# Rearranging loads and side work in an encoder-layer kernel: transform spectra and twiddles per frequency group, filter work out of the out-projections, filter network first, first loads in stages

## The chip, the cores and the metric

The kernel runs on all eight cores of one Trainium2 chip, one batch element per core, without any traffic between cores. The metric is the device time of the slowest core, in microseconds (us). A program on all eight cores has a second, slower state in some executions, in which the cores of one die, or of both, show a lower granted clock and the time is some per cent longer. Each run is labelled fast or slow, and only fast runs, or the undisturbed die of a run, are compared here. Times of fast runs repeat within about 0.3%.

## The reference, cut to what matters

One encoder layer on `x` of 2048 tokens by 2048 channels per core:

```python
x = x + 0.5 * swiglu(rmsnorm(x), w_ff1_in, w_ff1_out)        # FF1, 5632 hidden
h = rmsnorm(x)
proj = h @ w_in                # q/k/v of 6 heads, Hyena's v/x1/x2, memory queries, 3 gates
y_a = dilated sliding-window attention(...)                   # 3 groups of 2 heads
y_b = hyena_mixer(...)         # twice: multiply by x1/x2 after a long FFT convolution
y_c = cross attention into 256 memory tokens
merged = sig(ga)*(y_a @ w_br_a) + sig(gb)*(y_b @ w_br_b) + sig(gc)*(y_c @ w_br_c)
x = x + merged @ w_out
x = rmsnorm(x + 0.5 * swiglu(rmsnorm(x), w_ff2_in, w_ff2_out))  # FF2, closing norm
```

The long convolutions use filters that a small network of sine layers makes from positions alone. Their spectra depend on weights only, so the kernel computes them beside FF1, long before they are used.

## The kernel before

The kernel is a recorder: Python calls append operations in program order, every operation gets the semaphore waits that its data needs, and each engine then runs its own operations in that order. DMAs that the code gives to `"sp"` go out on one queue, in order; if one of them has to wait, everything behind it waits too. `"pool"` issues the weight loads.

Matmuls of the layer's large products are the main work. Everything else that needs the tensor engine (memory keys, filter spectra, attention, the Hyena operator) is a generator, a *side*, of which one step is recorded now and then between main matmuls. `rate` is the number of side steps per tick; a tick comes about every 8 to 16 main matmuls.

```python
    def tick(self):
        ...
        self.credit = min(self.credit + self.rate, 2.0) if self.sides else 0.0
        while self.credit >= 1.0 and self.sides:
            self.credit -= 1.0
            self.step()                       # one step of the first side in the list
```

The filter side: network, first transform step, and the second step that this excerpt shows. `T.tw` holds the twiddles, `T.ks` the spectra in HBM: a spectrum is the transform of a filter, and the twiddles are constant matrices that the second step of a transform, or of its inverse, multiplies with. The third component of a spectrum repeats the first.

```python
        seq2 = [(th, fg) for th in range(3) for fg in range(16)]
        def wload(i):
            th, fg = seq2[i]
            P.dma("sp", tw[i % 3][:], T.tw[fg][:, 0:3, :])
            P.dma("sp", W[i % 4]..., T.vk[o][th][:, 8 * fg:8 * fg + 8]...)
        for i, (th, fg) in enumerate(seq2):
            ... 4 matmuls into one bank ...
            wload(i + 3)
            P.store(0, T.ks[o][th][fg][:, 0:2, :], k_[:])
            P.store(0, T.ks[o][th][fg][:, 2, :], k_[:, 0, :])
            yield
```

The Hyena side, for each of two orders: a first step, 48 products (3 channel blocks `th` by 16 frequency groups `fg`) with a forward and an inverse part, and the inverse's last step (`last`) with 24 tiles. "Twiddle phase" below means the 48 products of an order. `W` is the result of the first step, `K` a spectrum, `Z` what the last step reads, `zz` its result.

```python
    W = bufs(P, "f_W", 4, [128, 2, 256], BF16, B)
    tw = bufs(P, "f_tw", 4, [128, 6, 128], BF16, B + 4 * KB)
    K = bufs(P, "f_K", 4, [128, 3, 256], F32, B + 10 * KB)
    zz_ = ring(bufs(P, "f_zz", 2, [128, 512], F32, B + 24 * KB))

    def fload(o, i):
        th, fg = i // 16, i % 16
        P.dma("sp", W[i % 4][:], T.vu[o][th][:, 8 * fg:8 * fg + 8]...)   # 128 KB
        P.dma("sp", K[i % 4][:], T.ks[o][th][fg])                        # 384 KB
    def tload(i):
        P.dma("sp", tw[i % 4][:], T.tw[i % 16])                          # 192 KB
    ...
        for i in range(50):                       # order(o)
            if i < 48:
                q.append((i, fwd(o, i)))
                yield
            if i >= 2:
                n, Y = q.pop(0)
                inv(o, n, Y)                      # stores 128 KB
                yield
            fload(o, i + 3)
            tload(i + 2)
    ...
        def zl(c6):                               # last(o): rows of 128 bf16, 256 bytes
            for part in range(2):
                P.dma("sp", Z[c6 % 2][:, part], T.vz[o][th][part][:, :, cc * 128:(cc + 1) * 128])
        for n, (c6, tb) in enumerate(its):        # 24 tiles
            ... 8 matmuls of 128 columns ...
            P.stt(zz[:], ps[:, bank, :], 2.0 / NFFT, v[:], ALU.mult, ALU.add)
            if o == 0:
                P.tt("dve", zz[:], zz[:], x[:], ALU.mult)
                P.store(1, T.z1[c6][:, tbs(tb)], zz[:])      # zz is busy until this lands
            ld(n + 3)                             # two loads of 256 KB
            yield
```

The start, and where the sides run in FF1:

```python
        for i in range(8):
            xload(i)                              # x tiles, 256 KB each
        W1.issue(2)                               # 2nd and 3rd FF1 weight tile, 1 MB each
        ... three weight tiles by four token blocks ...
        P.side("memkv", side_memkv(C, P, T, SIDE))
        P.side("filter", side_filter(C, P, T, SIDE))
        P.rate = 1.0                              # in in-projections and out-projections
```

## Time and profile before

| | |
|---|---|
| time, median of the runs | 6,091 us (6,084 to 6,103, four fast runs) |
| matmul work at full pace | about 5,605 us |
| lost on the slowest core | about 496 us |

*Lost* is used throughout: the length of a stage less its matmuls at full pace. A stage runs from the first matmul of its kind to the first of the next. The full pace is read from dense stretches: 465 matmuls of 512 columns in 100 us, 0.215 us each (over 4,640 such matmuls in a row it is 0.2158 us, and the losses in the tables below are reckoned with that); shorter matmuls count by their columns, with a floor of 0.06 us. The few fp32 matmuls are counted by their columns too, although the trace records 0.6 to 0.9 us for one of 512 columns, and so show a little as lost. Busy time of the tensor engine hides these losses, because a slow matmul is busy too.

Lines of the page of the kernel before. The last line counts DMA packets; the one before it has the granted clock of the tensor engine in tenths, in 40 slices of the span:

```profile
span 6101.1 us, 79583 instructions; the slowest of 8 cores (6032.7 to 6101.1 us)
PE 5767.4 (95%) x27356; PEld 2659.6 (44%) x27356; DVE 2166.2 (36%) x3185; ACT 1251.0 (21%) x2064; POOL 753.6 (12%) x876
PEclk9999999999999999999979989999999999999999
DMA packets 505331, 792.29 MB, mean 130 GB/s; under 512 B 94151, under 2 KB 274119, under 8 KB 493639
```

The windows view of the kernel before, core 4. Columns: stretch in us and its length, busy us (and instructions) of PE, weight loads, DVE, ACT, POOL, then granted clock, mean busy share of the DMA engines, GB/s. The stretches are FF1's first out-projection, its second in-projection, the q/k projection, the gate stage that holds most of the Hyena side, a dense stretch, and within the gate stage's surroundings the first twiddle phase and the first last step:

```profile
514.00:798.00 284.00, 258.69 (x1172) 114.01 (x1172) 85.02 (x128) 35.11 (x60) 7.91 (x15) 0.96 0.96 264
798.00:1295.00 497.00, 485.81 (x2317) 222.29 (x2315) 185.97 (x283) 99.56 (x171) 8.44 (x16) 0.99 0.65 169
2276.00:2517.00 241.00, 206.57 (x979) 92.85 (x977) 150.16 (x224) 130.14 (x218) 89.59 (x83) 0.95 0.40 87
2837.00:3720.00 883.00, 719.39 (x3643) 356.95 (x3642) 371.17 (x550) 199.76 (x337) 226.29 (x281) 0.88 0.70 181
3800.00:3900.00 100.00, 100.00 (x465) 45.36 (x464) 43.80 (x64) 13.21 (x21) 5.27 (x10) 1.00 0.41 94
2754.00:3039.00 285.00, 243.94 (x1247) 125.00 (x1245) 148.98 (x216) 64.36 (x109) 96.98 (x127) 0.93 0.76 205
3039.00:3181.00 142.00, 75.06 (x473) 40.30 (x472) 45.94 (x68) 45.92 (x80) 10.74 (x12) 0.76 0.79 183
```

The out-projection has its DMA engines busy 96% of the time; the gate stage takes 883 us for 3,643 matmuls, and its clock is 0.88 on average. Most of this low clock is a consequence of gaps and not their cause: the Trainium skill, "TensorE: Matmul & The Clock Gate", Part 1, says that the clock falls to half after an idle window and needs a busy one to come back, and this trace agrees (0.76 in the last step with its many gaps, 1.00 in the dense stretch; core 4 has 260 us at 0.5 in all). The exception is a stretch from 3,551 to 3,713 us in which cores 4 and 5 ran mostly at 0.812, a value that no other core of this run shows. Who the tensor engine waited for, from the waits view (us in total, times, longest):

```profile
PE P L225 <- DVE f_zz_246 L249: 32.1, 8, 16.5
PE P L225 <- DMA f_tw_220<-c_tw: 27.2, 9, 6.5
PE P L225 <- DVE f_zz_247 L249: 21.9, 4, 7.1
PE P L225 <- DMA h_W_124<-vk_s: 19.0, 8, 5.8
PE P L225 <- DMA h_W_123<-vk_s: 18.9, 7, 5.6
PE P L225 <- DMA f_Z_236<-vz_s: 18.1, 5, 9.4
...
PE P L225 <- ACT q_sq_159 L240: 17.3, 2, 16.5
```

`f_tw` are the twiddles (70 us over the four buffers), `h_W` the filter side's inputs, `f_zz` and `f_Z` belong to the last step, `q_sq` is the start of the q/k stage, where the cos/sin tables come late.

### The profile page before, as it was taken

What the parts mean: (1) busy time and instruction counts of PE and PEld (TensorE: products, weight loads), DVE (VectorE), ACT (ScalarE), POOL (GpSimd) and SP (SyncE); (2) the same over time, 40 slices, a digit from 0 to 9 for tenths busy, and PEclk for the clock granted to TensorE, in tenths of its full rate; (3) what the DMA queues carried; (4) which work ended last, traced back from release to release, by engine and by line L of the source; (5) the groups of instructions that cost most, each with busy time, mean ns of one, the idle gap of its engine ahead of it and who ended that gap; (6) DMA issues with size and microseconds to landing.
All of it is one profiled execution on the core that took longest, in us unless ns stands there. A gap on an engine that the chain in (4) does not pass through costs nothing.

```text
span 6101.1 us, 79583 instructions; the slowest of 8 cores (6032.7 to 6101.1 us)
## 1 busy us (share of the span) xinstructions
PE 5767.4 (95%) x27356; PEld 2659.6 (44%) x27356; DVE 2166.2 (36%) x3185; ACT 1251.0 (21%) x2064; POOL 753.6 (12%) x876
## 2 busy tenths in 40 slices
PE   7999889999999998898858889999999999999998
PEld 3444444444444453444424434444444444444443
DVE  3345225322332216665434443422222122322325
ACT  3211112110002445542232211123000000000014
POOL 0000000000002303302303311023000000000015
PEclk9999999999999999999979989999999999999999
DMA  7327974687225714367777764455212642156334
GB/s 162 65 48 197 268 209 119 179 223 186 39 38 135 182 52 97 87 160 208 202 182 206 197 152 96 94 152 150 42 35 48 180 108 42 35 133 164 66 91 166
DMA packets 505331, 792.29 MB, mean 130 GB/s; under 512 B 94151, under 2 KB 274119, under 8 KB 493639
## 3 DMA queue, kind: packets, MB, share of 16 engines
q1 hardware_dynamic: 456472, 583.30, 31.4%
q0 software_dynamic: 47232, 203.44, 20.2%
q8 instruction: 226, 3.70, 0.3%
q14 instruction: 169, 1.38, 0.1%
q10 hardware_dynamic: 1232, 0.46, 0.0%
HBM read 730.40 MB, written 260.05 MB: 162 GB/s over the span
## 4 chain that ended last, share of the span: by engine, by line
PE 79%; DMA 10%; SPq 4%; DVE 3%; issue 2%; ACT 2%; POOL 0%; ACTq 0%; DVEq 0%; POOLq 0%
PE P L225 79%; SPq L267 3%; DMA h_W_123<-vk_s 1%; DMA f_tw_220<-c_tw 1%; DMA xT_s<-a_xr_70 1%; DMA h_W_124<-vk_s 1%; DMA f_tw_218<-c_tw 1%; DMA z_s<-f_zz_247 1%; DMA xT_s<-a_xr_72 1%; DMA f_tw_219<-c_tw 0%; DMA x_in_77<-xt 0%; DMA f_tw_221<-c_tw 0%; DMA xT_s<-a_xr_69 0%; DMA z_s<-f_zz_246 0%; DMA vu_s<-f_stg_1_209 0%
## 5 line engine op out<-in xcount | busy, mean ns | idle before, releaser
L225 PE MATMUL P<-HT,a_w_0_62 128*128 128x512 bf16 x2816 | 626.7, 380 | 0.0
L225 PE MATMUL P<-HT,b_w_0_282 128*128 128x512 bf16 x2816 | 611.5, 379 | 0.0
L225 PE MATMUL P<-HT,b_w_1_283 128*128 128x512 bf16 x2816 | 611.4, 379 | 0.0
L225 PE MATMUL P<-HT,a_w_1_63 128*128 128x512 bf16 x2688 | 595.3, 379 | 0.0
L225 PEld LDWEIGHTS P<-HT,b_w_0_282 128*128 128x128 bf16 x2816 | 275.9, 98 | 332.2 <-issue 0.6
L225 PEld LDWEIGHTS P<-HT,b_w_1_283 128*128 128x128 bf16 x2816 | 275.2, 98 | 332.6
L225 PEld LDWEIGHTS P<-HT,a_w_0_62 128*128 128x128 bf16 x2816 | 275.8, 98 | 330.2 <-issue 10.8
L225 PEld LDWEIGHTS P<-HT,a_w_1_63 128*128 128x128 bf16 x2688 | 262.3, 98 | 311.1 <-issue 3.7
L225 PE MATMUL P<-HT,x_w_128 128*128 128x512 bf16 x1344 | 325.7, 394 | 0.0
L225 PE MATMUL P<-a_gT,a_w_0_64 128*128 128x512 bf16 x1408 | 316.4, 383 | 5.7 <-DVE a_xr_72 L249 2.8
L225 PE MATMUL P<-a_gT,a_w_1_65 128*128 128x512 bf16 x1408 | 318.2, 384 | 1.8 <-DMA a_w_1_65<-w_ff_out 1.8
L225 PE MATMUL P<-HT,x_w_129 128*128 128x512 bf16 x1344 | 319.2, 388 | 0.0
L225 PE MATMUL P<-HT,x_w_130 128*128 128x512 bf16 x1280 | 315.8, 397 | 0.0
L225 PE MATMUL P<-HT,x_w_131 128*128 128x512 bf16 x1280 | 311.3, 393 | 0.5 <-DVE m_m_259 L243 0.5
L225 PE MATMUL P<-b_gT,b_w_0_284 128*128 128x512 bf16 x1056 | 230.5, 379 | 0.0
L225 PE MATMUL P<-b_gT,b_w_1_285 128*128 128x512 bf16 x1056 | 230.5, 379 | 0.0
L225 PEld LDWEIGHTS P<-a_gT,a_w_0_64 128*128 128x128 bf16 x1408 | 138.8, 99 | 173.5 <-issue 13.9
L225 PEld LDWEIGHTS P<-a_gT,a_w_1_65 128*128 128x128 bf16 x1408 | 139.3, 99 | 168.7 <-issue 10.3
L225 PEld LDWEIGHTS P<-HT,x_w_128 128*128 128x128 bf16 x1344 | 135.6, 101 | 159.2 <-issue 33.1
L225 PEld LDWEIGHTS P<-HT,x_w_129 128*128 128x128 bf16 x1344 | 133.1, 100 | 152.2 <-issue 21.8
L225 PEld LDWEIGHTS P<-HT,x_w_130 128*128 128x128 bf16 x1280 | 129.4, 102 | 149.9 <-issue 31.2
L225 PEld LDWEIGHTS P<-HT,x_w_131 128*128 128x128 bf16 x1280 | 128.1, 101 | 147.3 <-issue 30.5
(889 smaller groups left out, 6478.5 us busy)
## 6 DMA issues: line engine op xcount, KB each, us to landing
b_w_0_282<-w_ff_in POOLq DMA_DIRECT2D x22, 1024.0 KB, 8.3
b_w_1_283<-w_ff_in POOLq DMA_DIRECT2D x22, 1024.0 KB, 8.3
a_w_1_63<-w_ff_in POOLq DMA_DIRECT2D x21, 1024.0 KB, 9.3
a_w_0_62<-w_ff_in POOLq DMA_DIRECT2D x21, 1024.0 KB, 9.1
x_w_128<-w_in POOLq DMA_DIRECT2D x21, 512.0 KB, 7.3
x_w_129<-w_in POOLq DMA_DIRECT2D x21, 512.0 KB, 8.0
x_w_130<-w_in POOLq DMA_DIRECT2D x20, 512.0 KB, 6.6
x_w_131<-w_in POOLq DMA_DIRECT2D x20, 512.0 KB, 7.3
```

The costliest lines, as they stand in the source:

```text
L225: self.add("pe", lambda e: e.matmul(out, lhsT=lhsT, rhs=rhs, start=start, stop=stop), r=(lhsT, rhs), w=(out,))
L267: self.add(q, lambda e: e.dma_start(out=out, in_=in_), r=(in_,), w=(out,), dma=True, shared=shared)
```

## The change

Its intent: move fewer bytes in the Hyena side, in longer rows, with fewer loads that a matmul waits for; run filter work only where the DMA engines have room; get the first projection going sooner; use the idle start for the filter network. The diff, cut to its core:

```diff
 # filter side: groups outermost, one twiddle load and one store per spectrum
-        seq2 = [(th, fg) for th in range(3) for fg in range(16)]
+        seq2 = [(fg, th) for fg in range(16) for th in range(3)]
-                P.dma("sp", tw[i % 3][:], T.tw[fg][:, 0:3, :])
+                if th == 0:
+                    P.dma("sp", tw[fg % 2][:], T.tw[fg][:, 0:3, :])
-            P.store(0, T.ks[o][th][fg][:, 0:2, :], k_[:])
-            P.store(0, T.ks[o][th][fg][:, 2, :], k_[:, 0, :])
+            P.store(0, T.ks[o][fg, th], k_[:])
 # Hyena side
-    W = bufs(P, "f_W", 4, [128, 2, 256], BF16, B)
-    tw = bufs(P, "f_tw", 4, [128, 6, 128], BF16, B + 4 * KB)
-    K = bufs(P, "f_K", 4, [128, 3, 256], F32, B + 10 * KB)
+    W = bufs(P, "f_W", 2, [128, 2, HYW], BF16, B)            # HYW: all 768 channels
+    tw = bufs(P, "f_tw", 2, [128, 6, 128], BF16, B + 6 * KB)
+    K = bufs(P, "f_K", 4, [128, 2, 256], F32, B + 9 * KB)
-        P.tt("dve", tb[:], pv, k[:, 1:3, :], ALU.mult)
+        P.tt("dve", tb[:, 0, :], pv[:, 0, :], k[:, 1, :], ALU.mult)
+        P.tt("dve", tb[:, 1, :], pv[:, 1, :], k[:, 0, :], ALU.mult)
-        zp = zp_()
+        zp = zp_[fg % 2]
...
-        P.store(1, T.vz[o][th][:, 8 * fg:8 * fg + 8]..., zp[:])
+        if th == 2:
+            P.store(1, T.vz[o][:, :, 8 * fg:8 * fg + 8]..., zp[:]...)
-                for part in range(2):
-                    P.dma("sp", Z[c6 % 2][:, part], T.vz[o][th][part][:, :, cc * 128:(cc + 1) * 128])
+                P.dma("sp", Z[n % 2]..., T.vz[o][th][:, :, 8 * bh:8 * bh + 8, :]...)   # 4 KB rows
                 q.append((i, fwd(o, i)))
+                kload(o, i + 3)
+                if i % 3 == 2:
+                    wload(o, i // 3 + 2)
                 yield
...
                 inv(o, n, Y)
+                if n % 3 == 2:
+                    tload(n // 3 + 2)
                 yield
-            fload(o, i + 3)
-            tload(i + 2)
 # start: the network's first layer among the x tiles, weights 2 and 3 only after x tiles 10 and 15
-        W1.issue(2)
+        P.side("mlp", side_mlp(C, P, T, A + 24 * KB, hh3b))
+        P.step()
...
+        W1.issue(1, also=(C.HT[:, 10, 0:512],))
+        W1.issue(1, also=(C.HT[:, 15, 0:512],))
...
+        P.drain("mlp")                          # its other two layers, all at once
 # FF1: side steps in the in-projections alone
-        P.rate = 1.0
+            P.tag = "ff1.in";  P.rate = 0.87
+            P.tag = "ff1.out"; P.rate = 0.0
 # q/k stage: V is loaded behind the cos/sin tables, attention starts two steps later
-        load_v(P, T, V)
+    load_v(P, T, V)                             # inside mix_qk, after the tables
```

## The prediction

> **What bounds the kernel now.** TensorE. In dense stretches of the windows view (after 3,720 us) 465 matmuls of 512 columns fit into 100 us, 0.215 us each, at granted clock 1.000. All matmuls of the timeline at that pace make about 5,605 us of the 6,101 us span (slowest core, 4). The other ~496 us are idle TensorE and half clock. By stage core 4 loses: before the first projection matmul 38 us; FF1's first in-projection 15; first out-projection (514 to 798 us) 44; second in-projection 24; start of q/k 42; gate stage with the Hyena work (2,837 to 3,720 us) 245, and 16 before it; tail 28. Undisturbed cores lose 200 to 215 us in the gate stage: cores 4 and 5 ran 150 us of it at clock 0.812.
>
> **Causes.** In the first out-projection the DMA engines are 94 to 102% busy (windows, 600 to 800 us), and the waits view has 38 us on filter spectra loads (h_W). In the gate stage it has 70 us on twiddle loads (f_tw), 54 on f_zz, 25 on f_Z. Gaps also halve the clock (mean 0.79 in 3,000 to 3,100 us), as the Trainium skill, "TensorE: Matmul & The Clock Gate", Part 1, says of idle windows; this trace agrees. The inverse transform's last step reads 256-byte runs: 26,000 of 37,000 packets in 3,024 to 3,182 us are under 512 B, the least that "DMA: Bandwidth & Descriptors", Specifications, asks for.
>
> **What the change does, priced.** TensorE work is the same (5,618 us counted in both programs).
> 1. Start: only 4 MB of x and the first weight tile precede the first projection; the next two tiles wait. First projection: 40.6 us becomes about 28. The filter network's later layers form a serial knot (2 us of DVE per block, 4 to 6 us of TensorE idling), repaid by its first layer moving into the idle start. Gain 12.
> 2. Filter work leaves the out-projections; 32.5 us of its matmuls move into in-projections, where DMA is 20 to 50% busy. 44 + 24 us of loss become about 8. Gain 60.
> 3. cos/sin tables load before V: the 16.5 us wait under q_sq mostly goes. Gain 14.
> 4. Hyena, per frequency group: K falls from 3x384 to 3x256 KB, twiddles from 3x192 to 192 KB, three stores become one; 2.5 MB become 1.7 MB. A twiddle load has three steps (about 6 us) of lead instead of two (4 us), against 5 to 6 us median to landing. 106 us of loss there become about 30. The last step's reads become 4 KB runs, but it still moves 1 MB per 2 us step, so it stays DMA-bound: 85 + 38 us become about 70. Expected gain 105, not the ideal 129. Cost: one more DVE product per step, off the chain.
>
> Sum: about 190 us, nearly all on the critical path, because TensorE's chain is the span.
>
> **Predicted: 5,905 us; 5,840 to 5,980 eight times in ten. Faster by over 2%: 0.84; within 2%: 0.14; slower: 0.02.**
>
> **What would show it.** First projection before 32 us; first out-projection about 210 us instead of 283; no h_W entry above 10 us in the waits view; f_tw below 20 us; packets under 512 B from 94,000 to about 45,000; gate stage 720 to 760 us instead of 883; ff2 unchanged.
>
> **What would make it wrong.** Twiddle waits becoming waits for K or W on the one in-order load queue; the filter knot stalling TensorE over 15 us; filter traffic delaying in-projection weights; denser matmuls bringing more of the 0.812 clock.

## The result, and the profile after

The changed kernel took 5,903 and 5,914 us in its two fast runs; two more runs were slow (one die at a clock of 0.81 and 0.85). The ratio of the fast runs to those of the kernel before is 0.970 (95% interval 0.967 to 0.973). Ratios are the mean time of one kernel's fast runs over that of the other's of the same rounds, so they are not quite the ratio of medians that are quoted. The lines that answer to those of before:

```profile
span 5901.2 us, 78600 instructions; the slowest of 8 cores (5877.6 to 5901.2 us)
PE 5712.2 (97%) x27356; PEld 2650.1 (45%) x27356; DVE 2178.8 (37%) x3308; ACT 1251.7 (21%) x2074; POOL 752.7 (13%) x876
PEclk9999999999999999999989999999999999999999
DMA packets 408365, 748.18 MB, mean 127 GB/s; under 512 B 39175, under 2 KB 174087, under 8 KB 396679
```

The windows view of the changed kernel, core 5, for the same stages in the same order:

```profile
528.00:735.00 207.00, 207.00 (x961) 93.84 (x960) 44.90 (x66) 0.40 (x1) 7.91 (x15) 1.00 0.74 203
735.00:1210.00 475.00, 475.00 (x2252) 216.10 (x2251) 184.21 (x279) 90.95 (x155) 8.44 (x16) 1.00 0.51 130
2224.00:2446.00 222.00, 204.31 (x979) 92.59 (x977) 148.87 (x224) 130.21 (x218) 89.09 (x80) 0.98 0.40 94
2754.00:3520.00 766.00, 676.79 (x3660) 347.81 (x3659) 389.66 (x648) 201.51 (x342) 229.48 (x286) 0.93 0.68 181
3600.00:3700.00 100.00, 100.00 (x466) 45.34 (x464) 43.53 (x63) 13.46 (x22) 5.28 (x10) 1.00 0.42 96
2698.00:2939.00 241.00, 226.79 (x1228) 120.38 (x1226) 150.32 (x259) 61.89 (x105) 98.93 (x129) 0.97 0.72 185
2939.00:3068.00 129.00, 81.03 (x471) 41.34 (x470) 45.45 (x67) 46.44 (x81) 7.82 (x10) 0.76 0.79 203
```

The out-projection has lost nothing any more, and the first twiddle phase is 44 us shorter with the same number of matmuls within 2%. The first last step is hardly shorter: 129 us against 142, with its clock still at 0.76. The waits view of the changed kernel:

```profile
PE P L225 <- DVE f_zz_240 L249: 19.1, 7, 8.9
PE P L225 <- DMA h_z<-c_zT: 17.0, 1, 17.0
PE P L225 <- DVE f_zz_241 L249: 14.2, 5, 4.5
...
PE P L225 <- DMA a_w_1_63<-w_ff_in: 5.3, 1, 5.3
...
PE P L225 <- DMA f_tw_216<-c_tw: 4.8, 3, 3.3
...
PE P L225 <- DMA f_tw_215<-c_tw: 2.9, 4, 1.0
```

Twiddle waits fell from 70 to 8 us and there is no `h_W` entry left. New are `h_z` (the filter network's table, at the very start) and a second FF1 weight tile that comes late. The other signs that the forecast named came too: packets under 512 B fell to 39,175, and the table has the first projection at 29 us, the first out-projection at 207 us, the gate stage at 755 us (median) and no change in FF2.

By stage, median of the eight cores from the traces, length in us and in brackets what is lost of it:

| stage | before | changed | best of the experiments |
|---|---|---|---|
| start, to the first projection matmul | 40.0 (37.5) | 29.0 (24.7) | 30.0 (26.6) |
| FF1, first in-projection | 473.7 (15.7) | 496.8 (30.8) | 469.7 (14.7) |
| first out-projection | 283.1 (44.0) | 207.2 (0.0) | 207.2 (0.1) |
| second in-projection | 489.9 (18.9) | 475.6 (9.8) | 476.5 (10.0) |
| second out-projection | 210.7 (1.9) | 207.2 (0.0) | 207.2 (0.0) |
| third in-projection | 386.8 (0.0) | 421.9 (3.3) | 437.3 (7.1) |
| q/k projection | 240.6 (42.1) | 223.9 (25.4) | 223.4 (24.9) |
| Hyena projection, second half | 191.7 (19.8) | 179.2 (9.0) | 182.5 (12.3) |
| gates of branches A and C, with the Hyena side | 851.4 (213.0) | 754.6 (114.5) | 677.1 (37.1) |
| everything after | unchanged within 5 us | | |
| third out-projection, memory queries and V, Hyena projection's first half | changed by 3 us or less each | | |

The Hyena side's phases, in the same way, add the detail that the stages hide:

| | twiddles, order 0 | last step, order 0 | twiddles, order 1 | last step, order 1 |
|---|---|---|---|---|
| before | 278.7 (54.6) | 134.1 (78.6) | 251.4 (48.1) | 83.0 (37.2) |
| changed | 237.9 (14.3) | 123.8 (68.8) | 211.1 (7.3) | 61.6 (15.4) |

### The profile page after: what moved, and what is told of

It is laid out like the page before. It is cut to its first block, busy times and chain, and to the rows that moved or that the text cites. A ratio compares the mean times of both kernels' runs of the same rounds, so it can differ in the third digit from the quotient of the medians.

```text
span 5901.2 us, 78600 instructions; the slowest of 8 cores (5877.6 to 5901.2 us)
## 1 busy us (share of the span) xinstructions
PE 5712.2 (97%) x27356; PEld 2650.1 (45%) x27356; DVE 2178.8 (37%) x3308; ACT 1251.7 (21%) x2074; POOL 752.7 (13%) x876
## 2 busy tenths in 40 slices
DMA packets 408365, 748.18 MB, mean 127 GB/s; under 512 B 39175, under 2 KB 174087, under 8 KB 396679
## 4 chain that ended last, share of the span: by engine, by line
PE 87%; DMA 7%; DVE 3%; ACT 1%; issue 1%; POOL 0%; SPq 0%; DVEq 0%; ACTq 0%; POOLq 0%
PE P L225 87%; DMA z_s<-f_zz_241 1%; DMA xT_s<-a_xr_70 1%; DMA xT_s<-a_xr_73 0%; DMA xT_s<-a_xr_72 0%; DMA xT_s<-a_xr_71 0%; DMA hyx_s<-y_uc_191 0%; POOL R L243 0%; DMA f_tw_216<-c_tw 0%; SPq L267 0%; DMA f_tw_215<-c_tw 0%; DMA f_zv_232<-z_s 0%; DMA vu_s<-f_stg_0_207 0%; DMA vz_s<-f_zp_229 0%; DMA xT_s<-a_xr_69 0%
## 5 line engine op out<-in xcount | busy, mean ns | idle before, releaser
L225 PE MATMUL P<-a_gT,a_w_0_64 128*128 128x512 bf16 x1408 | 311.1, 382 | 5.1 <-DMA a_w_0_64<-w_ff_out 5.1
L225 PE MATMUL P<-a_gT,a_w_1_65 128*128 128x512 bf16 x1408 | 307.8, 379 | 1.3 <-DMA a_w_1_65<-w_ff_out 1.3
```

What stands on the lines that cost most here:

```text
L225: self.add("pe", lambda e: e.matmul(out, lhsT=lhsT, rhs=rhs, start=start, stop=stop), r=(lhsT, rhs), w=(out,))
```

## The experiments

Twelve kernels ran, all correct against the reference. Whole-kernel times of fast runs are few, because many runs fell in the slow state; the stages of a trace, mostly over four to eight undisturbed cores (two in h_tw48lead), carry most verdicts. The kernel before took 6,052 to 6,103 us in its fast runs on the different chips, and the changed kernel itself ran on the first chip alone, so whole-kernel times from different rounds compare only within some 50 us.

### Parts undone, one at a time

**u_hyena.** The changed kernel with the old Hyena side, and the spectra stored as before.

```diff
-def side_hyena(...):  ... the changed one ...
+def side_hyena(...):  ... the one of before, with T.vu, T.vz, T.ks shaped as before ...
-            P.store(0, T.ks[o][fg, th], k_[:])
+            P.store(0, T.ks[o][th][fg][:, 0:2, :], k_[:])
+            P.store(0, T.ks[o][th][fg][:, 2, :], k_[:, 0, :])
```

> The changed kernel with the Hyena part alone put back (three-component spectra, twiddles per product, 256-byte rows in the inverse's last step). Theory: this part is worth about 105 us, nearly all in the gate stage: gate stage about 850 us again on the median core instead of 755, whole kernel about 6,005 us, ratio to the kernel before about 0.986; FF1 stages as in the changed kernel within 10 us. Rival (the gate stage got shorter because the stages before it hand over in a better state, not because of the loads): gate stage below 800 us.

Two fast runs: 6,003 and 6,006 us. The profiled run was slow on die 0; on the four undisturbed cores the gate stage took 850.0 us against 754.6 and the Hyena projection's second half 187.9 against 179.2, together 104 us. The theory holds: the gain goes and comes with the Hyena part itself; the stages before it, which this run keeps as changed, did not make it. The ratio was a miss: 0.992 against the one fast run of the kernel before in these rounds (6,052 us), where 0.986 was expected. The waits view of core 4 of this run has the old waits back:

```profile
PE P L225 <- DMA f_tw<-c_tw: 58.5, 22, 6.9
PE P L225 <- DVE f_zz L249: 44.5, 13, 20.2
```

**u_filter.** Filter work in the out-projections again, with the filter's own traffic still cut.

```diff
-            P.rate = 0.87      # in-projections
-            P.rate = 0.0       # out-projections
+        P.rate = 1.0           # once, before the loop
```

> The changed kernel with filter work allowed in the out-projections again (one step per tick everywhere), its loads still cut to one twiddle per group and one spectrum store. Theory of place (the out-projection's own x traffic and the filter's traffic together are more than the DMA engines carry): first out-projection loses 30 to 45 us again beyond its matmuls, kernel 30 to 45 us slower than the changed one. Rival of amount (the cut in the filter's own traffic did it): loss under 12 us there, kernel within 12 us of the changed one.

The first out-projection took 274.9 us and lost 42.4, as before the change; fast runs were 5,934, 5,936 and 5,967 us. Over all of FF1 the median core was 40 us slower than the changed kernel (39 without cores 0 and 1, which ran 300 us of it at a clock of 0.812). So the place is worth 40 us. That the filter's smaller traffic is worth nothing does not follow: since the network is done earlier here, this out-projection holds all 192 matmuls of the first order's second transform step, against 116 in the kernel before, and loses no more. No run has the old traffic in the new place. (The edit also raises the rate in the in-projections from 0.87 to 1.0.) The windows view of an undisturbed core (6), for this stage, shows the DMA engines as full as in the kernel before:

```profile
525.00:800.00 275.00, 246.91 (x1177) 116.18 (x1175) 56.86 (x87) 33.45 (x57) 8.45 (x16) 0.96 0.92 259
```

**u_loadv.** V ahead of the tables again.

```diff
+        load_v(P, T, V)        # before the q/k stage
-    load_v(P, T, V)            # in it, after the tables
-    for _ in range(4):
+    for _ in range(2):
```

> The changed kernel with the V loads ahead of the cos/sin tables again and attention starting two steps sooner. Theory: the q/k stage becomes about 17 us longer (224 to 241 us on the median core) and the kernel about 17 us slower. Rival (the wait only moves to the attention that needs V): kernel within 5 us.

The profiled run was slow on die 0. On die 1 the q/k stage was 236.8 us (223.9 in the changed kernel), the first half of the Hyena projection 130.4 (127.7), its second half 173.7 (179.2). So 13 us came back where expected, 3 more right after, and 5.5 were returned later, probably because attention that starts two steps sooner leaves less behind: 10 us net. The theory holds for the stage and is two thirds right for the kernel. The one fast run (5,907 us) can't show 10 us.

**u_weights.** The second and third weight tile at once.

```diff
+        W1.issue(2)
-        W1.issue(1, also=(C.HT[:, 10, 0:512],))
-        W1.issue(1, also=(C.HT[:, 15, 0:512],))
```

> The changed kernel with the second and third FF1 weight tiles loaded at once again. Theory A (holding them back is what brought the first projection from 40 to 29 us): first projection at 36 us or later, no wait for the second tile, start plus first in-projection within 5 us of the 526 us of the changed kernel, because the 5 us wait for the second tile goes in return. Theory B (the x loads are held by the filter network's first step in VectorE's order, not by the weights): first projection moves by less than 4 us and the stage gets about 5 us shorter.

The first projection started at 40.2 us instead of 29.0, and start plus first in-projection took 529.8 us instead of 525.8: theory A. Holding the weights back brings the first matmul 11 us forward and 4 us in the end. Fast runs were 5,902, 5,904 and 5,910 us, no different from the changed kernel.

### What in the Hyena side did it

The change did three things to the twiddle phases at once: 256 KB less per product, loads that cover a group instead of a product, and more lead for each. Four runs separate them.

**h_bytes** puts the bytes back as loads that nothing reads.

```diff
             P.dma("sp", K[i % 4][:], T.ks[o][i // 3, i % 3])
+            P.dma("sp", more[i % 4][:], T.hyx[i % 4][:, tbs(i % 4)])     # 256 KB
```

> The changed kernel, and beside every spectrum load a further load of 256 KB that nothing reads: the bytes that the change took out of the two twiddle phases are back, and no matmul waits for them. In the changed kernel these phases lose 22 us beyond their matmuls (238 and 211 us long), in the kernel before 103 us (279 and 251). Theory of bytes (fewer bytes, so shorter landings, so no stalls): the loss is back at 70 us or more. Theory of deadlines (one twiddle load per group with three steps of lead instead of one per product with two): loss under 45 us.

The two phases lost 86 us (49.0 + 37.1), of 103 in the kernel before and 22 in the changed one. Fast runs were 5,956 to 5,974 us, ratio 0.982. This is what the theory of bytes expected.

**h_tw48** loads twiddles once per product again, two steps ahead.

```diff
-    tw = bufs(P, "f_tw", 2, [128, 6, 128], BF16, B + 6 * KB)
+    tw = bufs(P, "f_tw", 4, [128, 6, 128], BF16, zoff)
-                if n % 3 == 2:
-                    tload(n // 3 + 2)
                 yield
+            tload(i + 2)                        # tw[i % 4] <- T.tw[i // 3]
```

> The changed kernel with the twiddles loaded once per product again, in four buffers and issued two steps ahead as before; spectra, inputs and stores stay as changed. It adds 128 KB per product, half of what the run with dead loads adds. Theory of deadlines: twiddle waits of 40 us or more in the waits view and a loss of 60 to 90 us in the two phases. Theory of bytes: at most half of the loss that the dead loads bring.

The phases lost about 61 us on the four undisturbed cores (32.8 + 28.8), with half of the bytes of h_bytes. That is more than half of what h_bytes lost above the changed kernel (39 of 64 us), so neither theory alone fits both runs. The waits view, first of h_bytes, then of h_tw48 (core 3):

```profile
PE P L225 <- DMA f_tw<-c_tw: 54.0, 16, 8.1
```

```profile
PE P L225 <- DMA f_tw<-c_tw: 37.5, 24, 4.4
```

In both it is the twiddles that are late: few and long waits in the first, many and short in the second. The question is then whether they are late because the engines are full or because the load has too little lead. Two more runs changed only the lead.

**h_tw48lead** is h_tw48 with six buffers (the diff is cut, and against h_tw48). Counted in the code, two steps of lead become six, not the eight that the expectation says.

```diff
-    tw = bufs(P, "f_tw", 4, ...)      tload(i + 2)
+    tw = bufs(P, "f_tw", 6, ...)      tload(i + 4)
```

> Twiddles per product again, as in the run that lost 61 us in the two phases (22 in the changed kernel) with 37 us of twiddle waits, the same bytes, but six buffers and four products (about eight steps) of lead instead of two. Theory (per-product loads cost mostly through their short lead): twiddle waits under 5 us, loss 22 to 35 us. Rival (the 128 KB more per product cost by themselves): loss stays above 50 us, the waits turn up at W or K.

The profiled run was slow, but cores 4 and 5 went slow only at 3,337 us, after both twiddle phases. There the phases lost 16.5 us (12.7 + 3.8), with no wait for twiddles, W or spectra in the waits view of core 4. The windows view of that core has the first phase: as many bytes as in h_tw48, DMA engines 84% busy, and the phase as short as in the changed kernel.

```profile
2693.00:2931.00 238.00, 225.68 (x1249) 120.61 (x1247) 150.60 (x260) 64.10 (x109) 100.25 (x131) 0.98 0.84 220
```

So 128 KB more per product costs nothing, if the twiddles are issued in time. Its one fast run was 5,900 us, against 5,974 for the one of h_tw48 (on another chip, where the kernel before ran within 15 us of the same time). The phases account for 45 of these 74 us; the rest may be the scatter of single runs.

**h_bytelead** is h_bytes with a third twiddle buffer (the diff is cut, and against h_bytes).

```diff
-    tw = 2 buffers; tload(n // 3 + 2)
+    tw = 3 buffers; tload(n // 3 + 3)
```

> The run with the dead loads again (256 KB more per product in the twiddle phases, which then lost 86 us, 54 us of it waiting for twiddles), now with a third twiddle buffer, so that a twiddle load has about nine steps of lead instead of three. Theory: bytes cost time because they make every landing later than its lead; then the twiddle waits vanish (under 5 us) and the loss of the two phases falls to 40 us or less although the bytes are the same. Rival (the DMA engines carry no more, whatever the lead): twiddle waits turn into waits for W or K, and the loss stays above 65 us.

Neither number came. The waits for twiddles vanished, as the theory said, but the loss only fell from 86 to 57 us (33.3 + 23.5), and the next load in line was late instead (13 to 25 us by core; the profiled core 4 below). Fast runs took 5,934 and 5,948 us.

```profile
PE P L225 <- DMA f_W<-vu_s: 24.9, 9, 4.6
```

The windows view of the same core has the first phase:

```profile
2702.00:2964.00 262.00, 231.01 (x1233) 120.61 (x1232) 152.76 (x262) 63.64 (x108) 100.35 (x131) 0.96 0.88 217
```

The DMA engines were 87 and 94% busy in the two phases, against 72% in the changed kernel, and W's 384 KB took a median of 9.8 us to land, against 4.7 to 6.5. With 256 KB more per product the engines are near full, and lead for one stream moves the wait to another. Taken together: bytes and lead are one question, whether a load lands before its use. In these runs lead was enough at 84% busy engines, and not near 90%, where fewer bytes are needed as well. The busy share alone does not set when a load lands: W took a median of 9.1 us in h_bytes at 83%, and 5.3 us in h_tw48lead at 84%. By an estimate the kernel before would have needed both: its first phase shows 76% over 285 us, and the same traffic in the changed kernel's 241 us would be 90% (76 x 285 / 241). The change gave both; no run gave the kernel before more lead alone.

**h_zruns**: the last step's reads as 256-byte rows again, same bytes.

```diff
-                P.dma("sp", Z[n % 2]..., T.vz[o][th][:, :, 8 * bh:8 * bh + 8, :]...)
+                for part in range(2):
+                    for cc in range(2):
+                        cs = slice(cc * 128, cc * 128 + 128)
+                        P.dma("sp", Z[n % 2][:, part, :, cs], T.vz[o][th][part][:, 8 * bh:8 * bh + 8, cs])
```

> The changed kernel with the inverse's last step reading 256-byte runs again, the same bytes. Today the two last steps lose 69 and 15 us (124 and 62 us long); before 79 and 37. Theory of packets: the second comes back to about 35 us and the first to about 79, kernel about 25 us slower. Rival (only the bytes and the order count): both within 6 us of today.

The last steps took 140.3 and 79.5 us (124 and 62 in the changed kernel) and lost 85.0 and 33.3, and fast runs took 5,937 us. The theory of packets holds, with a little more than it forecast. The count of short packets is nearly the kernel before's (94,151) again:

```profile
DMA packets 455022, 748.19 MB, mean 126 GB/s; under 512 B 88903, under 2 KB 223815, under 8 KB 443335
```

The Trainium skill, "DMA: Bandwidth & Descriptors", Specifications, gives 512 B as the least size for full rate. This run agrees: 49,700 more packets under 512 B, at the same bytes, cost 34 us in the two last steps. (It also issues four loads where the changed kernel has one, so a part of the 34 us may be issue.)

### What still bounds the last step

**r_zz4.** In the changed kernel's first last step the DMA engines are 79% busy, so bandwidth is not used up. The waits view of VectorE in that stretch (2,939 to 3,068 us) names another cause:

```profile
DVE f_zz_241 L249 <- DMA z_s<-f_zz_241: 29.7, 7, 6.7
DVE f_zz_240 L249 <- DMA z_s<-f_zz_240: 17.7, 3, 11.7
```

A result buffer can't be written again before its store has landed, and there are two of them. The run gives it four:

```diff
-    zz_ = ring(bufs(P, "f_zz", 2, [128, 512], F32, B + 24 * KB))
+    zz_ = ring(bufs(P, "f_zz", 2, [128, 512], F32, B + 24 * KB) + bufs(P, "f_zzb", 2, [128, 512], F32, B + 31 * KB))
```

> The changed kernel with four instead of two result buffers in the inverse's last step. The forecast held this step to be bound by DMA bandwidth, but in the changed kernel's profile VectorE waits 47 us in it for the store of the buffer that it wants to write again. Theory of buffers: the first order's last step shortens from 124 to 105 us or less, kernel 15 to 25 us faster. Rival (bandwidth): under 6 us shorter, the wait turns up as one for loads.

The first last step fell from 123.8 to 99.3 us, the second, which stores nothing, stayed at 62.0. One fast run: 5,885 us. VectorE's waits for stores fell from 47 to 9 us, and the windows view now shows the step at bandwidth, which it had not been:

```profile
DVE f_zz L249 <- DMA z_s<-f_zz: 5.3, 2, 4.1
DVE f_zzb L249 <- DMA z_s<-f_zzb: 3.3, 1, 3.3
2948.00:3047.00 99.00, 68.08 (x461) 36.84 (x459) 45.41 (x67) 46.18 (x80) 6.65 (x7) 0.88 0.95 265
```

### The start

**s_late.** The filter network's first step behind the ninth x tile, its later layers spread over weight tiles 3 to 5 (with it the rate in the rest of the first in-projection is 0.9 instead of 0.87). In the changed kernel the trace of the tensor engine shows three places where the new start loses time:

```profile
16.96 3.64 PE L225 MATMUL P<-h_z,h_fw_95 33*64 33x512 f32 x4 [16.96 <-DMA h_z<-c_zT]
...
45.15 5.28 PE L225 MATMUL P<-HT,a_w_1_63 128*128 128x512 bf16 x12 [5.33 <-DMA a_w_1_63<-w_ff_in]
...
143.74 1.93 PE L225 MATMUL P<-h_z,h_fw_97 64*64 64x512 f32 x2 [1.41 <-ACT h_z L240]
```

The columns are start, length, instruction, and in brackets the idle time before it and what ended it. The first line is the network's first layer waiting for its table, with VectorE, and so the reloading of x buffers, behind it; the second is the held-back weight tile; the third one of four waits in the two layers that run all at once between 132 and 155 us.

```diff
+    yield                                     # in side_mlp, after its loads are issued
-                if tb == 0 and c % 2:
+                if tb == 0 and c % 2 and c > 8:
                     P.step()
-        P.drain("mlp")                        # after weight tile 2
+                if j == 6:
+                    P.drain("mlp")            # steps run at rate 1.0 in tiles 3 to 5
```

> The changed kernel with the filter network's first step moved behind the ninth x tile (until now VectorE's first instruction waits for that step's matmul, which waits 17 us for its table, and no x buffer is reloaded before 20 us), and its later layers spread over weight tiles 3 to 5 instead of run at once. Theory: first projection at 22 to 26 us instead of 29, no knot at 132 to 155 us (12 us lost there now); start plus first in-projection about 15 us shorter after taking off the filter work that moves on to later stages; kernel 10 to 18 us faster than the changed one. Rival (x bandwidth sets the start): first projection stays at 28 to 30 us and only the knot's 8 to 10 us are won.

The first projection came at 30.1 us, not earlier: x buffers were reloaded from 12 us on instead of 20, but x then arrived no faster. The rival was right about the start. The first in-projection lost 13.9 us instead of 30.8, more than the knot, since the second weight tile was in time as well (that wait is gone from this run); 4 us came back as loss in the third in-projection, where filter work moved. Start to third in-projection, the median core gained 10 us. Fast runs were 5,896 and 5,902 us; the ratio, 0.972 (0.968 to 0.976), is against few runs and can't tell 10 us.

### What helped, with three parts that no run tried alone

**best.** The four result buffers, a second yield per tile of the last step so that main matmuls fill it, s_late, the third twiddle buffer, and the first branch weights issued two projection units sooner. The second yield and the branch weights were never run alone, nor was the third twiddle buffer in the changed kernel.

```diff
             ld(n + 3)
             yield
+            yield
...
+        if jh == 16:
+            C.wb()                            # WB.issue(2)
```

> The changed kernel with four result buffers and two yields per tile in the inverse's last step, the network's steps as in the run before, the first branch weights loaded two units before they are needed, and three twiddle buffers. Sum of the terms: last steps lose 60 us less than the 84 now, start and knot 15, branch weights 8, twiddles 5: about 5,820 us against 5,903, ratio to the kernel before about 0.957. If main work can't fill the last step (the loads still come later than two steps), only half of the 60 comes: about 5,850.

Four fast runs took 5,816 to 5,822 us; the ratio is 0.959 (0.957 to 0.961), against 0.970 for the changed kernel on its own chip and 0.972 for s_late in the same rounds. The last steps lost 17.2 and 2.1 us instead of 68.8 and 15.4; r_zz4, with the four buffers alone, lost about 60 in the two together, so an estimated 41 us of the gain belong to the second yield. They are not shorter (108 and 85 us): more main work runs inside them, and the plain gate work that followed the Hyena side shrank from 110 to 31 us. The windows view of this kernel's gate stage (core 3, up to the last 16 us), and the longest wait of the whole kernel:

```profile
2740.00:3417.00 677.00, 643.32 (x3624) 336.18 (x3622) 393.46 (x652) 201.54 (x343) 229.05 (x287) 0.98 0.77 207
```

```profile
PE P L225 <- ACT x_sq L240: 20.9, 7, 12.4
```

The clock is at 0.98 instead of 0.93, and the longest wait that is left is the start's.

## Why the prediction was right or wrong

The forecast was 5,905 us and the fast runs gave 5,903 and 5,914. The mechanism, a kernel whose time is the tensor engine's work plus its gaps, held: the matmul count is the same, and each shortened stage shortened the kernel. Some terms were off and cancelled, so that the total came within 10 us is partly luck: of the four gains that follow, the forecast had 12, 60, 14 and 105 (191 us), and the losses by the table moved by -2, 52, 17 and 109 (176 us); the medians of the fast runs moved by 182 us, where the forecast took some 196 from the 6,101 us of the profiled core.

1. *"Start ... Gain 12"* failed. The first projection came at 29 us, as forecast (28), but start and first in-projection together lost 55 us of 526, against 53 of 514 before. The knot lost 12 us instead of the forecast 4 to 6 (132 to 155 us of the trace, half of it at a low clock), and the held-back second weight tile came 5.3 us late, followed by more time at half clock. Both were only partly in the forecast. u_weights shows that holding back is worth 4 us net; s_late shows that both the knot and the late tile could be avoided.
2. *"Filter work leaves the out-projections ... Gain 60"* was close. From the first out-projection to the third in-projection the loss fell by 52 us (64.8 to 13.1, sums of the table). u_filter shows 40 us in FF1 to be the place alone.
3. *"cos/sin tables load before V ... Gain 14"* was right in the stage (17), but 5.5 us of it were returned to the attention that starts later, as u_loadv shows: 10 net.
4. *"Hyena ... Expected gain 105"* was right: 109 us by the table (105 without cores 4 and 5 of the kernel before, which had the 0.812 clock), 104 by u_hyena. The split was off. The twiddle phases went from 103 to 22 us of loss where the forecast had 106 to 30. The last steps went from 116 to 84 where it had 123 to 70, because the step *"so it stays DMA-bound"* was wrong: the engines were 79% busy, and two result buffers, each held until its store had landed, were the bound. r_zz4 shows it. The 123 was core 4's; its 0.812 stretch began only at 3,551 us, after the first last step (it ended at 3,181 us), so most of the difference to 116 is one core against the median of eight.
5. Of the things said to make it wrong, the one-queue worry (waits moving to K or W) did not occur in the changed kernel, but did in h_bytelead. More of the 0.812 clock did not come either: the profiled run of the changed kernel shows none on any core. In the kernel before, 152 us of it made the profiled core 4 an estimated 28 us slower (152 x 0.188); the table's gate stage holds little of it (851 us, and 847 without cores 4 and 5).

Not settled: which part of the last steps' gain is row length and which the fewer issues; what the filter's smaller traffic is worth; whether more lead alone would have helped the kernel before; and how much of the first two runs' difference of 11 us is chance.

## What to carry to other kernels

Before cutting a load's bytes, ask what it misses: twiddle loads with a median landing of about 4 us were often late with two steps of lead (about 2.6 us each) in h_tw48, and never with six in h_tw48lead; where the DMA engines were not full (84%), buffers for more lead were worth as much as fewer bytes. A buffer that is stored is busy until the store has landed; a ring of two of them looked like a bandwidth limit here, and the DMA engines' busy share told the two apart (79% against 95%). Side work belongs where its own resource is free: moving it out of the stage that filled the DMA engines gained 40 us without one operation less, and slowing a DMA-bound side so that main matmuls fill it gained an estimated 41 us more.

## What the Trainium skill lacked or had wrong

- "TensorE: Matmul & The Clock Gate", section "Back-to-back issue gap", gives about 131 ns per matmul of 512 columns as the sustained rate of weight-load and matmul pairs. No dense stretch of the traces of the kernel before, the changed one and best is faster than 0.2158 us each; that agrees with the 215.7 ns that the same page, "Wait — 56ns, not 53.3ns?", measures.
- The same page, Part 1, has the limiter take a die to 13/16 of the clock within 5 to 20 us once three of its cores run dense matmuls. Here all eight cores of the changed kernel's fast profiled run had no record of it, with dense stretches of 100 us and more at a clock of 1.00. In other fast profiled runs it lasted only on pairs of cores (4 and 5 for 150 us in the kernel before; 0 and 1 for 300 us and, much later, 2 and 3 for 170 us in u_filter); elsewhere it came in pieces of at most 91 us a core in all. In one slow run of the changed kernel a whole die had a mean clock of 0.81.
- "DMA: Bandwidth & Descriptors" prices a transfer by size (about 2 us plus bytes) and says that HBM access gets slower at high load. It doesn't say how the landing of a large load grows with other traffic: the same 384 KB load landed after a median of 4.7 to 6.5 us with the engines 72% busy (the changed kernel), 5.3 us at 84% (h_tw48lead), 9.1 us at 83% (h_bytes) and 9.8 us near 90% (h_bytelead).
- No page names, as a limit to plan for, that a result buffer is held until its store has landed: 47 us of VectorE's waits in one 129-us stretch were that, and two more buffers of 256 KB shortened it by 24 us.
